# Moving the normalised tokens to the upper end of the SBUF partition, and the context, mixed and MLP features down beside the weight tiles

## The chip, the cores and the metric

The kernel runs on one core of a Trainium2 chip. The metric is the device time of one execution in microseconds (us). The kernel before took 2857.2 us (median of three runs, 2851.56 to 2862.92).

## The reference

One layer of a diffusion backbone over 512 latent tokens and 256 context tokens of width 2048, all in float32. Cut to what matters:

```python
sh1, sc1, g1, sh2, sc2, g2 = split(silu(c) @ w_ada + b_ada)           # modulation vectors
u_lat = rmsnorm(x) * (1 + sc1) + sh1                                  # 512 tokens ("normalised tokens")
u_ctx = rmsnorm(ctx) * (1 + csc1) + csh1                              # 256 tokens ("context")
p_lat, p_ctx = u_lat @ w_in, u_ctx @ w_in                             # 8192 columns
a_lat = hgrn2(p_lat[:, :5120], p_ctx[:, :5120])                       # 8 heads, both directions
y_lat = hyena(p_lat[:, 5120:])                                        # long convolution by transform matrices
x = x + g1 * (concat(a_lat, y_lat) @ w_out)                           # "mixed features"
u2 = rmsnorm(x) * (1 + sc2) + sh2
x = x + g2 * (square(relu(u2 @ w_mlp1)) @ w_mlp2)                     # hidden width 8192 ("MLP features")
out = rmsnorm(x)
```

## The kernel before, in words

TensorE works in three products per float32 product. `wsplit` (L198) and its like split each operand into a rounded part `hi` and the exact rest `lo`, and every product is hi·hi + hi·lo + lo·hi: `mm3` (L249 to L252), or the three lines L1022 to L1024 and L1102 to L1104. Each of these matmuls loads a stationary tile of 128 x 128 and streams a moving tile of 512 columns (256 for the context) past it; the accumulators are PSUM banks.

A weight tile `raw` (512 KB, 128 x 1024) is loaded by SyncE's queue, rounded by ScalarE (`whi`, L202) and split by VectorE (`wlo`, L149), three in flight at each step (`Stream`). The stages follow each other:

- head (to about 160 us): modulation of x, filter of the long convolution; the normalised tokens `uT0` to `uT15` are made, one tile of 4 KB per partition for each block of 128 features (hi 2 KB, lo 2 KB).
- Hyena (to about 540 us): projections of `uT`, transforms with the matrices `mat`, `mati`, `fsd`, `ff`.
- HGRN (to about 1228 us): for each head a query and a gate (`project`, of `uT` alone) and three projections of both `uT` and the context `uc` (`project2`, three `uT` matmuls and three `uc` matmuls in turn).
- output projection (to about 1406 us): weights stream as the moving side, the mixed features `mix0` to `mix15` are the stationary side; `OUT_PLAN` goes through mix8 to 15 (`Y_ROWS`) and mix0 to 7 (`A_ROWS`) in turn.
- MLP (to about 2836 us): eight rounds; in each, first `u2 @ w_mlp1` (L1080, stationary `whi`/`wlo`, moving `u2`), then `h @ w_mlp2` (L1102 to L1104, stationary `h`, moving `whi`/`wlo`), 384 matmuls each.

In `mm3(ps, wh, wl, xh, xl, ..)` the second argument of `pe.matmul` is the stationary side and the third the moving side. The profile's operand pairs don't tell the roles, which are taken from the code: in rows of L250 to L252 with `uT`, `u` or `uc`, that tile is moving; in rows of L1022 to L1024 and L1102 to L1104, `mix` and `h` are stationary; of `mat,pq` the moving one is `mat`; of `fsd,mat` and `ff,mat` the stationary one is `mat`.

SBUF is shared out by pools, which are stacked from the left (low addresses) or from the right (high addresses) of each partition. The pools of this change: A holds `uT`, later mix0 to 7, later `u2` (and for a while the odd filter groups' `ff`); YM holds `uc`, later mix8 to 15, later `h`; W holds `raw`, `whi`, `wlo`. M holds `mat`, Y `mati`, `ue`, `uo` and `pq`.

```python
    MP = pool("M", side=right)
    mat = MP.tile([P, 2, 4, 2, 256], F32R, name="mat")
    AP_ = pool("A")
    WP = pool("W")
    HP = pool("H", side=right)
```

Of the kernel before, what the change touches and what calls it, by code (L numbers as in the profile page):

```python
# [29 lines left out]
RAW, WB = 3, 3  # weight tiles in flight as loaded and as split  # L30
MISC_QUEUE = "scalar"
NPRE, PRE_CTX = 2, 0  # heads whose query and gate come first; the one after which the context is prepared
K_QUEUE = "sync"
P_QUEUE = "gpsimd"
FILTER_AT = {0: (0, 1, 2, 3)}  # channel groups of the filter after a step of the modulation
# how far instructions move up or down in the order of issue
# [5 lines left out]
SIDE = 114  # weight tiles over which the later modulation vectors are spread  # L42
# [25 lines left out]
def stream_order():  # L68
    """Weight tiles of [128, 1024] in the order of their use: (weight, first row, first column, k blocks)."""
    r = []  # L70

    def half_cols(c0):
        r.extend(("w_in", hf * W, c0, 8) for hf in range(2))

    def pairs(w, rows, c0):
        r.extend((w, r0, c0, 2) for r0 in rows)

    for g in range(4):
        for n in range(3 if g == 0 else 0, 6):
            half_cols((5 + n // 2) * W + (2 * g + n % 2) * P)  # L80
    for h in range(NPRE):
        for part in (0, 4):
            half_cols(part * W + h * P)
    for h in range(H):
        for part in (1, 2, 3) + ((0, 4) if h >= NPRE else ()):
            half_cols(part * W + h * P)
    for ng, rows in OUT_PLAN:
        pairs("w_out", rows, ng * 512)
    for c in range(8):
        for f in (2 * c, 2 * c + 1):  # L90
            pairs("w_mlp1", range(0, D, 256), f * 512)
        for rep in range(1 if c < 7 else 2):
            for ng in range(4):
                pairs("w_mlp2", range(c * W, (c + 1) * W, 256), ng * 512)
    return r


def arrange(a):
    """The inputs as the kernel loads them: weights in tiles, vectors as columns."""
    f = np.float32  # L100
    k = constants()
    ada = a["w_ada"][0].reshape(P, 16, 6, D)
    order = list(dict.fromkeys(stream_order()))
    tiles = np.empty((len(order), P, 1024), f)
    for t, (w, r0, c0, nk) in zip(tiles, order):
        n = 1024 // nk
        t.reshape(P, nk, n)[:] = a[w][0][r0:r0 + nk * P, c0:c0 + n].reshape(nk, P, n).transpose(1, 0, 2)
    first = np.concatenate([a["w_in"][0][:, 5 * W:5 * W + 256], a["w_in"][0][:, 6 * W:6 * W + P]], axis=1)
    rows = lambda v: v.reshape(-1, P).T
    pad = lambda v: np.concatenate([v, np.zeros((P - v.shape[0],) + v.shape[1:], f)])  # L110
    twice = lambda v, axis: np.concatenate([v, v], axis=axis)
    fvec = np.stack([a["flt_b1"][0], a["flt_b2"][0], a["flt_freq"][0]], axis=1)
    head = [a["c"][0].reshape(P, 16), a["c_ctx"].reshape(P, 16), twice(fvec, 0), k["k_negt"], pad(a["flt_w1"][0]),
            pad(twice(a["flt_w2"][0], 1))]
    cols = [rows(a["b_ada"][0]), rows(a["norm1_g"][0]), rows(a["norm2_g"][0]),
            rows(a["hgrn_norm_g"][0]), rows(a["hy_conv_b"][0]), rows(a["hgrn_lb_logits"]), rows(a["hy_conv_w"][0]),
            rows(a["hy_bias"][0])]
    d = {"x": a["x"][0], "ctx": a["ctx"][0], "b_ada": a["b_ada"], "final_norm_g": a["final_norm_g"][None],
         "ada1": ada[:, :, 0:2].reshape(P, 8, 2, 2, 8, 256).transpose(4, 1, 0, 2, 3, 5).reshape(8, 8, P, 1024),
         "ada2": ada[:, :, 2:6].reshape(P, 16, 16, 512).transpose(2, 1, 0, 3),  # L120
         "first": first.reshape(8, 2, P, 384).transpose(0, 2, 1, 3).reshape(8, P, 768),
         "tiles": tiles, "head": np.concatenate(head, axis=1),
         "columns": np.concatenate(cols, axis=1),
         "flt_w3": twice(a["flt_w3"][0].reshape(64, 2, 4, 256).transpose(0, 2, 1, 3).reshape(64, 2, 1024), 0),
         "k_zt": k["k_zt"], "k_delta": k["k_delta"], "k_mats": k["k_mats"], "k_tri": k["k_tri"]}
    return {n: np.ascontiguousarray(v) for n, v in d.items()}
# [16 lines left out]
def body(nc, tc, A, out, stack, dbg, stop):  # L143
# [4 lines left out]
    right = "right"  # L148
# [31 lines left out]
    grow = DR.tile([2, D], F32, name="grow")  # L180
# [7 lines left out]

    MP = pool("M", side=right)
    mat = MP.tile([P, 2, 4, 2, 256], F32R, name="mat")  # L190
    AP_ = pool("A")
# [6 lines left out]
    def wsplit(raw, n=1024):  # L198
        """f32r parts of the first n columns: the rounded value and the exact rest."""
# [6 lines left out]
    class Stream:  # L206
        """Weight tiles [128, k, n], loaded and split ahead of their use."""
# [25 lines left out]
    class Side:  # L233
        """Tasks spread evenly over a number of weight tiles."""
# [19 lines left out]
    def rsqrt_small(v, scale, pl, tag, add=EPS):  # L254
        """v <- (v * scale + add) ** -0.5 for a few columns: square root, reciprocal and one Newton step."""
# [11 lines left out]
    def make_u(u, xp, t, scale, bias):  # L267
        """u[:, 0], u[:, 1] <- f32r parts of xp * scale + bias."""
# [4 lines left out]
    # ---------------- conditioning vectors  # L273
# [20 lines left out]
    def load_wa(p):  # L294
        """Modulation columns of pair p as eight tiles of two k rows: shift and scale, 256 columns each."""
# [9 lines left out]
    def load_k(p):  # L305
        """Rows of the first three projected blocks for k blocks 2 p, 2 p + 1."""
        raw = wraw()
        kdma(raw[:, 0:768], A["first"][p])
        return raw

    # ---------------- x: token tiles, normalised
# [3 lines left out]
    # ---------------- implicit filter of the long convolution (some tiles borrow the space of later uT blocks)  # L315
# [12 lines left out]
    def load_mats(dst, i0, n):  # L328
        """Transform matrices i0, i0 + 1, .. as pairs of f32r parts."""
# [7 lines left out]
    # the second layer comes out on both halves of the partitions, for two concurrent products with half of the rows  # L337
# [27 lines left out]
    def forward(banks, q, ut):  # L365
        """Sum q (cosine even, odd; sine even, odd tokens) of a token-major tile: [128 m, (2, 256 ch)]."""
# [18 lines left out]
    def filter_taps(g):  # L385
        """Taps of 256 channels, forward and backward, by token parity; the squares' sums go to rnf."""
# [34 lines left out]
    def filter_spectrum(g):  # L421
        """Transform of the taps of channel group g: sums and differences of the two directions."""
# [34 lines left out]
    # ---------------- modulation of x, two k blocks at a time  # L457
# [6 lines left out]
    def mod_pair(p):  # L464
        """Shift and gain of x and of the context for k blocks 2 p, 2 p + 1: four rows of the vectors at a
        time, each on its own strip of the array's columns."""
# [19 lines left out]
    def project_k(p):  # L486
        """Adds k blocks 2 p, 2 p + 1 to the first three projected blocks."""
# [28 lines left out]
    # lower bound of the forget gates: softmax over two logits  # L516
# [21 lines left out]
    # ---------------- modulation vectors of later stages  # L538
    def gemv(col0, fin, row):
        """Tasks of 512 columns from col0; fin gets four feature columns [128, 4], or with row a row [1, 512]."""  # L540
# [27 lines left out]
    def mod_vec(name, six, norm=None):  # L568
        """Column block `six` of the modulation, [128, 16]; with norm: norm * (1 + value)."""
# [13 lines left out]
    def mod_row(r, six):  # L583
        """Column block `six` of the modulation as row r of grow."""
# [25 lines left out]
    # ---------------- Hyena: projections, long convolution  # L610
# [14 lines left out]
    def hy_evac(g, n, ps, cv, ueo):  # L625
        """Convolved block n (v, v, x1, x1, x0, x0) of channel group g; u = x1 * v goes token-major."""
# [90 lines left out]
    # ---------------- HGRN: both directions of a head at a time  # L717
    YM = pool("YM", side=right)  # context, later the mixed features of w_out, later the hidden features
# [22 lines left out]
    def view(ap, h):  # L741
        """Column-major order of the latent grid for the upper heads."""
# [20 lines left out]
    # queries and gates of the first heads run while the context is prepared  # L763
    for h in range(NPRE):
        mdma(qscr[h], query(h))
        mdma(gscr[h], gate(h))
        if h == PRE_CTX:
            # context: normalised and modulated, feature-major
# [24 lines left out]
    def project2(ps, pc):  # L793
        """Latent and context columns; the context follows two blocks behind."""
# [12 lines left out]
    def head(h):  # L807
        dirs = []
        for di, nm in enumerate("fb"):
# [10 lines left out]
            # cumulative log decay within chunks; for the context the sum over the tokens still to come  # L820
# [33 lines left out]
        # values  # L854
# [15 lines left out]
        # state that the context leaves  # L870
# [23 lines left out]
        # scores, transposed, two chunks at a time on the two halves of the array's columns; both directions  # L894
        # join block-diagonal matrices of two chunks
# [15 lines left out]
        for i in range(NCH):  # L911
            ns = i, NCH - 1 - i
            if i < NCH - 1:
                us = [0, 0]
                for di, n in enumerate(ns):
                    b_ = n % 2  # each half of the rows has its own bank
# [16 lines left out]
        # gate and readout  # L933
# [37 lines left out]
    # ---------------- output projection, residual, second norm; token-major  # L971
# [19 lines left out]
    def residual(pl, ps, i, ng, ssq):  # L991
        """x1 += row * ps for token tile i and column group ng; the squares' sum goes to ssq."""
# [8 lines left out]
    def rstd(pl, v, n, tag):  # L1001
        """[128, n, 4] sums of squares -> [128, n] reciprocal roots."""
# [48 lines left out]
    # ---------------- MLP  # L1051
# [8 lines left out]
    def final(i0):  # L1060
        """Output of token tiles i0, i0 + 1."""
# [62 lines left out]
```

## Time and profile before

| | |
|---|---|
| time, median of three runs | 2857.2 us (2851.56, 2857.20, 2862.92) |
| span of the profiled execution | 2851.5 us; the fastest of the three runs took 2851.56 us |
| TensorE matmul busy | 2794.1 us, 98% of the span, 13444 matmuls |
| TensorE weight load busy | 2219.4 us, 78% |
| VectorE, ScalarE busy | 1399.7 us (49%), 926.7 us (32%) |
| DMA | 369.07 MB, mean 129 GB/s |
| chain that ended last | 91% TensorE |

A matmul's row has a start and a duration; the duration (0.39 us at 512 columns) holds its way through the array and overlaps the next one's. What a matmul costs in a stream is therefore read from start to start.

### The profile page before, as it was taken

To read this page: it belongs to the slowest core of one execution; us is meant where nothing else is said; L and a number is where in the kernel's file an instruction comes from. 1 tells how busy PE (TensorE), PEld (TensorE's weight loads), DVE (VectorE), ACT (ScalarE), POOL (GpSimd) and SP (SyncE) were. 2 spreads that over 40 slices of the span, in tenths; PEclk is the share of its full clock that TensorE was granted. 3 is DMA by queue.
4 is the path that set the end of the run, shared out by engine and by line. 5 is a ranking of instruction groups with operands and counts; after the bars stand their busy time and mean duration, and the time that the engine had idled before them with its cause. 6 is when DMAs were issued, how large, how long until landed. Compare 5 with 4: busy or idle time off the path is not lost.

```text
span 2851.5 us, 33241 instructions
## 1 busy us (share of the span) xinstructions
PE 2794.1 (98%) x13444; PEld 2219.4 (78%) x13444; DVE 1399.7 (49%) x2021; ACT 926.7 (32%) x1269; POOL 11.5 (0%) x26
## 2 busy tenths in 40 slices
PE   7999999999999999999999999999999999999997
PEld 2468788787888877878788888888888888888886
DVE  4447777655564656533434344243442434424446
ACT  5432222554344423522332131222312222122233
POOL 0000000000000000100000000000000000000000
PEclk9999999999999999999999999999999999999999
DMA  7576555713443354333232222322222222233245
GB/s 303 214 263 198 163 181 162 252 49 111 137 129 105 111 156 136 116 139 113 96 104 96 96 96 89 104 94 95 93 96 97 95 97 96 96 96 96 96 132 178
DMA packets 122405, 369.07 MB, mean 129 GB/s; under 512 B 13595, under 2 KB 13979, under 8 KB 120332
## 3 DMA queue, kind: packets, MB, share of 16 engines
q1 hardware_dynamic: 112608, 339.00, 36.5%
q10 hardware_dynamic: 7724, 18.78, 1.8%
q0 software_dynamic: 1920, 9.18, 0.9%
q8 instruction: 105, 1.72, 0.3%
q14 instruction: 48, 0.39, 0.0%
HBM read 353.52 MB, written 13.39 MB: 129 GB/s over the span
## 4 chain that ended last, share of the span: by engine, by line
PE 91%; DMA 4%; DVE 3%; ACT 1%; issue 1%; SPq 0%; DVEq 0%; ACTq 0%
PE bank L250 17%; PE bank L251 17%; PE bank L252 17%; PE bank L1103 8%; PE bank L1102 8%; PE bank L1104 8%; DMA ga<-ada_dram 2%; PE bank L1022 2%; PE bank L1023 2%; PE bank L1024 2%; PE bank L471 2%; PE bank L921 1%; PE bank L923 1%; DVE gacc L554 1%; PE bank L865 0%
## 5 line engine op out<-in xcount | busy, mean ns | idle before, releaser
L149 DVE TENSOR_TENSOR wlo<-raw,whi 128x1024 fp32r<-128x1024 f32 (+1 forms) x434 | 529.1, 1219 | 974.0 <-ACT whi L202 957.3
L202 ACT CAST whi<-raw 128x1024 fp32r<-128x1024 f32 (+1 forms) x434 | 453.7, 1045 | 1374.2 <-PE bank L251 656.6
L251 PE MATMUL bank<-uT,whi 128*128 128x512 f32 x1024 | 408.4, 399 | 0.0
L252 PE MATMUL bank<-uT,wlo 128*128 128x512 f32 x1024 | 406.7, 398 | 0.0
L250 PE MATMUL bank<-uT,whi 128*128 128x512 f32 x1024 | 406.7, 397 | 0.0
L1102 PE MATMUL bank<-whi,h 128*128 128x512 f32 x1024 | 404.7, 395 | 0.0
L1103 PE MATMUL bank<-wlo,h 128*128 128x512 f32 x1024 | 404.7, 395 | 0.0
L1104 PE MATMUL bank<-whi,h 128*128 128x512 f32 x1024 | 404.6, 395 | 0.0
L252 PE MATMUL bank<-u,wlo 128*128 128x512 f32 x1024 | 399.3, 390 | 0.0
L250 PE MATMUL bank<-u,whi 128*128 128x512 f32 x1024 | 399.1, 390 | 0.0
L251 PE MATMUL bank<-u,whi 128*128 128x512 f32 x1024 | 398.9, 390 | 0.0
L252 PEld LDWEIGHTS bank<-uT,wlo 128*128 128x128 f32 x1024 | 193.0, 189 | 50.5 <-issue 12.5
L1103 PEld LDWEIGHTS bank<-wlo,h 128*128 128x128 f32 x1024 | 192.1, 188 | 46.9
L1104 PEld LDWEIGHTS bank<-whi,h 128*128 128x128 f32 x1024 | 192.1, 188 | 46.8
L1102 PEld LDWEIGHTS bank<-whi,h 128*128 128x128 f32 x1024 | 192.0, 188 | 46.9
L250 PEld LDWEIGHTS bank<-u,whi 128*128 128x128 f32 x1024 | 192.3, 188 | 39.9 <-ACT u L270 0.3
L251 PEld LDWEIGHTS bank<-u,whi 128*128 128x128 f32 x1024 | 192.3, 188 | 39.7
L252 PEld LDWEIGHTS bank<-u,wlo 128*128 128x128 f32 x1024 | 192.4, 188 | 39.6
L250 PEld LDWEIGHTS bank<-uT,whi 128*128 128x128 f32 x1024 | 193.0, 189 | 36.2 <-issue 9.2
L251 PEld LDWEIGHTS bank<-uT,whi 128*128 128x128 f32 x1024 | 193.5, 189 | 32.9 <-issue 6.6
L554 DVE SCALAR_TENSOR_TENSOR gacc<-ga,sil,gacc 128x512 f32<-128x512 f32 x240 | 179.5, 748 | 65.5 <-DMA ga<-ada_dram 62.5
L250 PE MATMUL bank<-uc,whi 128*128 128x256 f32 x384 | 108.8, 283 | 1.1 <-ACT sf L814 1.1
(395 smaller groups left out, 2931.9 us busy)
## 6 DMA issues: line engine op xcount, KB each, us to landing
raw<-tiles_dram SPq DMA_DIRECT2D x426, 512.0 KB, 3.5
ga<-ada_dram SPq DMA_DIRECT2D x256, 256.0 KB, 3.5
wa<-ada_dram SPq DMA_DIRECT2D x64, 512.0 KB, 6.3
x<-x_dram SPq DMA_DIRECT2D x4, 1024.0 KB
kscr<-kt ACTq DMA_DIRECT2D x8, 512.0 KB
K<-kscr ACTq DMA_DIRECT2D x4, 1024.0 KB, 6.6
x<-x_dram POOLq DMA_DIRECT2D x4, 1024.0 KB, 9.3
out_dram<-x SPq DMA_DIRECT2D x16, 256.0 KB, 2.3
```

Of the source, the lines that this page charges most:

```text
L149: tt = lambda o, x, y, op: vec.tensor_tensor(out=o, in0=x, in1=y, op=op)
L202: act.copy(hi[:, :n], raw[:, :n])
L250: pe.matmul(ps, wh, xh, start=start, stop=False, skip_group_check=True)
L251: pe.matmul(ps, wh, xl, start=False, stop=False, skip_group_check=True)
L252: pe.matmul(ps, wl, xh, start=False, stop=stop_, skip_group_check=True)
L471: pe.matmul(gm[32 * j:32 * j + 32, :], sil[:, kk], w_[kk // 2][:, kk % 2].rearrange("p a n -> p (a n)"), start=kk < 4, stop=kk >= 12, skip ...
L554: vec.scalar_tensor_tensor(out=acc, in0=g, scalar=s, in1=acc, op0=ALU.mult, op1=ALU.add)
L1022: pe.matmul(ps, m[:, 0, sl], hi[:, k], start=first, stop=False, skip_group_check=True)
L1023: pe.matmul(ps, m[:, 0, sl], lo[:, k], start=False, stop=False, skip_group_check=True)
L1102: pe.matmul(psb[i], t[:, 0, sl], hi[:, k], start=first, stop=False, skip_group_check=True)
L1103: pe.matmul(psb[i], t[:, 0, sl], lo[:, k], start=False, stop=False, skip_group_check=True)
L1104: pe.matmul(psb[i], t[:, 1, sl], hi[:, k], start=False, stop=last, skip_group_check=True)
```

## The change

Pool A is opened first of the pools on the right side, so that it takes the top of the partition, and everything else on that side (M, H, Y, Q, R, E, F) moves down under it. W moves down into the place of A. YM is opened on the left side, right above W. Nothing else is changed but comments.

```diff
@@ body
+    AP_ = pool("A", side=right)
     MP = pool("M", side=right)
     mat = MP.tile([P, 2, 4, 2, 256], F32R, name="mat")
-    AP_ = pool("A")
     WP = pool("W")
     HP = pool("H", side=right)
@@ after close("Y"), close("M")
-    YM = pool("YM", side=right)  # context, later the mixed features of w_out, later the hidden features
+    YM = pool("YM")
     QP = pool("Q", side=right)
```

On all five engines the two programs have the same instructions in the same order with the same waits, 19049 in each; only the names and the addresses of tiles differ. The addresses of the built programs, in bytes from the start of the partition, and the rest that the first byte of the pool's large tiles leaves when divided by 64:

```
pool  tiles                         before            rest   after             rest
W     raw, whi, wlo, ga              86784 .. 131840    0     21248 ..  66304    0
A     uT; mix0-7; u2; ff (odd g)     21248 ..  86784    0    163808 .. 229344   32
YM    uc; mix8-15; h                196576 .. 229344   32     66304 ..  99072    0
M     mat                           212960 .. 229344   32    147424 .. 163808   32
Y     mati, ue, uo, pq              133088 .. 212960   32     67552 .. 147424   32
H     fsd, ff (even g), wa          139776 .. 212960   32     74240 .. 147424   32
```

The tiles in W, A and YM are each a multiple of 512 bytes long and the slices that matmuls read start at multiples of 512 bytes in them, so the rest of the pool is the rest of each operand. Pools Q, E, F and R keep their rests.

## Rows read from the trace of the kernel before

**Rows 1.** The page, parts 1, 2 and 4: busy time by engine, the span in 40 slices (tenths busy, granted TensorE clock), and the chain that ended last.

```profile
span 2851.5 us, 33241 instructions
PE 2794.1 (98%) x13444; PEld 2219.4 (78%) x13444; DVE 1399.7 (49%) x2021; ACT 926.7 (32%) x1269; POOL 11.5 (0%) x26
PE   7999999999999999999999999999999999999997
PEclk9999999999999999999999999999999999999999
PE 91%; DMA 4%; DVE 3%; ACT 1%; issue 1%; SPq 0%; DVEq 0%; ACTq 0%
```

**Rows 2.** Busy time in the stretches head, Hyena, HGRN, output projection, normalisation, MLP, end: length of the stretch, busy us (and instructions) of PE, PEld, DVE, ACT, POOL, granted clock, DMA share, GB/s.

```profile
0.00:156.00 156.00, 134.51 (x641) 62.76 (x641) 74.09 (x162) 74.55 (x108) 0.69 (x6) 0.99 0.70 262
156.00:540.00 384.00, 373.52 (x1829) 298.16 (x1829) 270.21 (x406) 117.25 (x164) 0.00 (x0) 1.00 0.62 202
540.00:1228.00 688.00, 684.96 (x3996) 553.47 (x3995) 391.84 (x658) 296.44 (x459) 8.19 (x15) 1.00 0.38 118
1228.00:1406.00 178.00, 177.16 (x772) 144.24 (x771) 58.00 (x63) 47.71 (x65) 2.62 (x5) 1.00 0.36 123
1406.00:1421.00 15.00, 7.93 (x43) 6.39 (x42) 11.72 (x29) 10.59 (x20) 0.00 (x0) 0.77 0.32 116
1421.00:2836.00 1415.00, 1415.00 (x6168) 1153.90 (x6168) 584.43 (x687) 378.54 (x450) 0.00 (x0) 1.00 0.31 101
2836.00:2851.00 15.00, 0.98 (x5) 0.46 (x3) 9.46 (x21) 1.65 (x5) 0.00 (x0) 0.67 0.42 140
```

**Rows 3.** The timeline of PE at the borders of two MLP stages: start, duration, engine, line, operands. Between the first border and the second lie the 384 matmuls of one `h @ w_mlp2`, between the second and the third the 384 of the next `u2 @ w_mlp1`.

```profile
1510.52 0.40 PE L252 MATMUL bank<-u,wlo 128*128 128x512 f32 x1
1510.75 0.39 PE L1102 MATMUL bank<-whi,h 128*128 128x512 f32 x1
...
1600.12 0.39 PE L1104 MATMUL bank<-whi,h 128*128 128x512 f32 x1
1600.34 0.39 PE L250 MATMUL bank<-u,whi 128*128 128x512 f32 x1
...
1687.16 0.40 PE L252 MATMUL bank<-u,wlo 128*128 128x512 f32 x1
1687.39 0.39 PE L1102 MATMUL bank<-whi,h 128*128 128x512 f32 x1
```

**Rows 4.** The timeline of PE in the output projection, first at matmuls whose stationary side is of mix8 to 15 (YM), then of mix0 to 7 (A), as `OUT_PLAN` orders them; ten matmuls from the first row of each pair to its second.

```profile
1237.89 0.39 PE L1024 MATMUL bank<-whi,mix 128*128 128x512 f32 x1
...
1240.22 0.40 PE L1022 MATMUL bank<-whi,mix 128*128 128x512 f32 x1
...
1289.88 0.39 PE L1023 MATMUL bank<-wlo,mix 128*128 128x512 f32 x1
...
1292.14 0.39 PE L1024 MATMUL bank<-whi,mix 128*128 128x512 f32 x1
```

**Rows 5.** The timeline of PE at matmuls of 256 columns that all stand on tiles of rest 32 on the stationary side: eleven with `ff` of filter group 3 (A) moving past `mat`, then twelve with `mat` moving past `pq`. The last row of each pair is the start of the matmul behind them.

```profile
149.50 0.28 PE L251 MATMUL bank<-ff,mat 128*128 128x256 f32 x1
...
150.78 0.39 PE L250 MATMUL bank<-uT,whi 128*128 128x512 f32 x1
...
253.37 0.28 PE L250 MATMUL bank<-mat,pq 128*128 128x256 f32 x1
...
254.81 0.28 PE L252 MATMUL bank<-mati,pq 128*128 128x256 f32 x1
```

**Rows 6.** The timeline of PE in two heads' projections: from the first row to the second three `uT` matmuls that lie between `uc` matmuls; from the third to the fourth nine `uc` matmuls of 256 columns without a `uT` one between them.

```profile
578.72 0.39 PE L250 MATMUL bank<-uT,whi 128*128 128x512 f32 x1
...
579.41 0.28 PE L250 MATMUL bank<-uc,whi 128*128 128x256 f32 x1
...
724.21 0.28 PE L250 MATMUL bank<-uc,whi 128*128 128x256 f32 x1
...
725.27 0.39 PE L250 MATMUL bank<-uT,whi 128*128 128x512 f32 x1
```

**Rows 7.** The page, part 5, the groups of matmuls and of weight loads: line, engine, operation, operands, count, then busy us, mean ns of one, idle us before them. Each group is one of three lines with the same count.

```profile
L251 PE MATMUL bank<-uT,whi 128*128 128x512 f32 x1024 | 408.4, 399 | 0.0
L1102 PE MATMUL bank<-whi,h 128*128 128x512 f32 x1024 | 404.7, 395 | 0.0
L250 PE MATMUL bank<-u,whi 128*128 128x512 f32 x1024 | 399.1, 390 | 0.0
L1022 PE MATMUL bank<-whi,mix 128*128 128x512 f32 x256 | 100.4, 393 | 0.8 <-DVE m L952 0.8
L1104 PEld LDWEIGHTS bank<-whi,h 128*128 128x128 f32 x1024 | 192.1, 188 | 46.8
L252 PEld LDWEIGHTS bank<-u,wlo 128*128 128x128 f32 x1024 | 192.4, 188 | 39.6
L250 PE MATMUL bank<-uc,whi 128*128 128x256 f32 x384 | 108.8, 283 | 1.1 <-ACT sf L814 1.1
```

**Rows 8.** The matmuls that read `uT`, in Hyena and in HGRN, and then those that read `uc`, in HGRN: stretch, length, busy us (and count), granted clock, DMA share, GB/s.

```profile
156.00:540.00 384.00, 302.00 (x1277) 1.00 0.62 202
540.00:1228.00 688.00, 478.41 (x1730) 1.00 0.38 118
...
540.00:1228.00 688.00, 189.20 (x1152) 1.00 0.38 118
```

**Rows 9.** Who waited for whom in Hyena: engine, what, on what, then us in total, times, longest.

```profile
DVE gacc L554 <- DMA ga<-ada_dram: 42.1, 28, 3.0
ACT whi L202 <- DMA raw<-tiles_dram: 10.1, 3, 4.4
```

## The prediction

> **What bounds the kernel now.** I read the busy times and the slices first [rows 1]: TensorE is busy 98% of the span, its clock stands at the full level (2.4 GHz) in every slice, and 91% of the chain that ended last is TensorE's. The reader is to see that nothing but the number of matmuls and what one costs can move this time by much. The windows by stage [rows 2] say where that holds: in the MLP (1415 us) PE has no idle time, in HGRN (688 us) 3 us, in the output projection (178 us) 1 us, in Hyena 10.5 us, in the head 21.5 us.
>
> Then I read the price of a matmul, start to start, in each stage, because a busy PE does not say at what pace it goes. One `h @ w_mlp2` goes from 1510.75 to 1600.34, 89.59 us for 384 matmuls or 233.3 ns each; the `u2 @ w_mlp1` behind it goes from 1600.34 to 1687.39, 87.05 us for 384 or 226.7 ns each [rows 3]. Both have 512 columns, both read weight tiles as one side, neither waits. The output projection shows the same two prices with only one thing exchanged: with mix8 to 15 as the stationary side ten matmuls take 2.33 us (233 ns), with mix0 to 7 they take 2.26 us (226 ns) [rows 4]. The moving side is `whi` and `wlo` in both, the lines are the same three. What differs is the pool: YM against A. In YM tiles start 32 bytes past a multiple of 64, in A on a multiple of 64. I call a tile of rest 32 *shifted*. A shifted stationary tile costs 6.6 ns per matmul of 512 columns.
>
> The load of the stationary tile itself is not longer: 188 ns with `h`, 188 ns with the weights [rows 7]. The price shows only in the pace of the stream.
>
> For the moving side the trace has a pair at 256 columns, both with a shifted stationary tile: with `ff` of A (not shifted) moving, 11 matmuls take 1.28 us, 116.4 ns each; with `mat` (shifted) moving, 12 take 1.44 us, 120.0 ns each [rows 5]. A shifted moving tile costs 3.6 ns there; I take 3.3 ns, half of 6.6, since 116.7 is half of the 233.3 of a shifted stationary tile at 512 columns, and 120.0 is one such step above it. By columns that is 6.6 ns at 512.
>
> **What the change does.** It removes, adds and moves no instruction and no wait; every engine has the same rows in the same order. It exchanges the rests: A becomes shifted, YM stops being shifted, all others stay as they are. So the sum is over matmuls that read A or YM. Counts are from [rows 7, 8].
>
> 1. `h @ w_mlp2`, 3 x 1024 matmuls, stationary side no longer shifted: 3072 x 6.6 ns = 20.3 us less. PE has no idle time there, so it is all on the path. The price is the row's own.
> 2. `u2 @ w_mlp1`, 3 x 1024 matmuls, moving side now shifted: at 6.6 ns, 20.3 us more, all on the path. This pairing (stationary tile not shifted, moving tile shifted, 512 columns) has no row. Lower bound 0: the pair of [rows 5] was taken beside a shifted stationary tile and may not hold without one; a gain is left out, since no row shows a shifted tile at a quicker pace than an unshifted one. Upper bound 9.0 ns: `uc` is shifted, moves past unshifted weights, and nine of its matmuls take 1.06 us, 117.8 ns each [rows 6]; against the 113.3 that half of 226.7 would be, that is 4.5 ns at 256 columns. I take 6.6, the value of the pair in which only the moving tile differs.
> 3. The output projection: 384 matmuls get an unshifted stationary side, 384 a shifted one, each 6.6 ns. Sum 0.
> 4. `uT` in Hyena's stretch: 1277 matmuls x 6.6 ns = 8.4 us. Here PE waits 10.5 us of 384, and the waits behind it are transfers (VectorE waits 42.1 us for the modulation weights `ga`, and its splits of weight tiles queue behind that [rows 9]). A slower PE gives the transfers time, so a part is absorbed: I take three quarters, 6.3 us. Bounds: 0 (all 8.4 lie under the 10.5 us) and 8.4.
> 5. `uT` in HGRN: 1730 matmuls, of which the 24 projections with context (3 for each of 8 heads, 16 blocks of 3 matmuls each) have 1152 and queries and gates 578. The 578 alone: 3.8 us. The 1152: 7.6 us, less what `uc` gains by not being shifted, 1152 x 3.3 ns = 3.8 us, so 3.8 us more. That gain is less sure: beside `uc` the three `uT` take 0.69 us, 230 ns each instead of 226.7 [rows 6], so the turn from one kind to the other costs something too, and stays.
> 6. `uT` in the head: 3072 - 1277 - 1730 = 65 matmuls, 0.4 us, hidden: PE is idle 21.5 of 156 us there. Without that cover it would cost these 0.4 us. What VectorE and ScalarE read and write at shifted places is taken as 0 too: in the MLP they are busy 584 and 379 of 1415 us [rows 2], so that they could take twice as long under the cover of PE.
>
> Sum: -20.3 + 20.3 + 0 + 6.3 + 3.8 + 3.8 = +13.9 us. The profiled execution had a span of 2851.5, the fastest of the three runs; on it the forecast is 2865. The median of the runs is 5.7 us above, so on the median it is 2871.
>
> **A rule that speaks against it.** The Trainium skill ("TensorE: Matmul & The Clock Gate", Part 2, on loading the stationary operand) says that PE has two independent SBUF read ports and that loading the next tile's weights doesn't steal read bandwidth from the running matmul. "SBUF — State Buffer" (Specifications) gives lines of 16 bytes, of which 32 and 64 are both multiples. By these two no start in question should matter and the sum would be 0, 2857. The trace disagrees for the stationary side: 233 against 226 ns [rows 4]. It has no row for the third case in step 2.
>
> **Rivals.**
>
> *A shifted moving tile costs nothing past unshifted weights.* Then steps 2, 4 and 5 fall away, with `uc`'s gain, and only step 1 stays: -20.3, 2837 on the median; faster. For it: no row shows this pairing against its own unshifted counterpart. Against it: `mat` against `ff` [rows 5], and `uc` [rows 6], which with only its moving side shifted goes no quicker (117.8) than `ff` with only its stationary side shifted (116.4). The point from which it decides: per ns of moving price steps 2, 4 and 5 come to 3.07 + 0.96 + 0.58 + 1.15 = 5.8 us, step 1 gives 20.3 and `uc` 3.8, so the sum falls below 0 where the price is under 24.1 / 5.8 = 4.2 ns (3.5 if `uc` gains nothing).
>
> *The moving price is per matmul, not per column*: 3.3 ns at 512 columns too. Then -20.3 + 10.1 + 3.2 + 1.9 + 0 = -5, 2852; no change that can be told.
>
> *The moving price is what `uc` shows*, 9.0 ns: -20.3 + 27.6 + 8.6 + 5.2 + 10.4 - 3.8 = +28, 2885; slower.
>
> *The start of a tile is not the cause at all.* Something that goes with `h` and mix8 to 15 (what else is written into that pool, say) makes the 6.6 ns and stays: 0, 2857. Against it: the same line of the code writes mix0 to 6 and mix8 to 15, and `h` is written and read by others; the slow ones share only the pool. A variant: it is not the rest by 64 but the upper half of the partition (all shifted tiles above lie from 133088 up). Then A, which goes up, pays the same as in my sum, YM gains the same, and `mati`, `ue` and `uo` come down and gain under 1 us: the forecast stays.
>
> **How the numbers follow.** Chances: my sum 0.45, moving side free 0.17, per matmul 0.13, as `uc` shows 0.15, no effect 0.10. About 0.5%, 14.3 us, is what a measurement of this kernel can tell from no change, and my sum ends right at it, so its chance is divided between same and slower. Slower: 0.15 + 0.27 = 0.42. Faster: 0.17. Same: the rest, 0.41. The range goes from the free moving side to the `uc` case, each with some us for the runs' scatter: 2835 to 2888; the likeliest case alone, with step 4 at its bounds and `uc`'s gain between 0 and 4.5 ns, is 2863 to 2877.
>
> **What would show it.** In the timeline of the changed kernel: `h @ w_mlp2` in 87.05 us per 384 matmuls (step 1), `u2 @ w_mlp1` in 89.6 (step 2; 87.05 if the moving side is free, 90.5 if it is as `uc` shows), output projection with mix0 to 7 at 233 ns and mix8 to 15 at 226 (step 3), `ff` of filter group 3 past `mat` at 120.0 instead of 116.4. Hyena's stretch should grow by less than 8.4 us, with PE idle for less than 10.5 (step 4), HGRN's by 7.6 us (step 5). I am wrong if the two MLP stages don't change places, above all if `u2 @ w_mlp1` keeps its 87.05.

## The result: slower by 6 us, not by 14

The kernel after takes 2861.63 us (median of 20 runs, 2857.96 to 2871.61), the kernel before on the same chips 2855.45 us (20 runs, 2851.42 to 2863.04). The ratio is 1.0026, 95% interval 1.0017 to 1.0035: 5 to 10 us slower, 0.3%, less than the 0.5% that the prediction called noise. The forecast was +13.9 us.

### The profile after

The page of the kernel after, parts 1 and 5, against [rows 1, 7]:

```profile
span 2864.3 us, 33241 instructions
PE 2808.1 (98%) x13444; PEld 2223.4 (78%) x13444; DVE 1399.2 (49%) x2021; ACT 927.0 (32%) x1269; POOL 11.5 (0%) x26
...
L250 PE MATMUL bank<-u,whi 128*128 128x512 f32 x1024 | 405.6, 396 | 0.0
...
L1102 PE MATMUL bank<-whi,h 128*128 128x512 f32 x1024 | 398.4, 389 | 0.0
```

The same instructions, the same share of PE, and the means of `u` and `h` have changed places (390 to 396 and 395 to 389). The timeline of PE at three MLP borders, against [rows 3]; from the first row to the second lies one `h @ w_mlp2`, to the third the next `u2 @ w_mlp1`:

```profile
1525.91 0.40 PE L1102 MATMUL bank<-whi,h 128*128 128x512 f32 x1
...
1612.95 0.40 PE L250 MATMUL bank<-u,whi 128*128 128x512 f32 x1
...
1702.56 0.39 PE L1102 MATMUL bank<-whi,h 128*128 128x512 f32 x1
```

87.04 and 89.61 us: the two products have exchanged their prices. So have the halves of the output projection. Ten matmuls of mix8 to 15, then ten of mix0 to 7, against [rows 4]:

```profile
1251.83 0.39 PE L1022 MATMUL bank<-whi,mix 128*128 128x512 f32 x1
...
1254.10 0.39 PE L1023 MATMUL bank<-wlo,mix 128*128 128x512 f32 x1
...
1291.67 0.39 PE L1022 MATMUL bank<-whi,mix 128*128 128x512 f32 x1
...
1294.01 0.39 PE L1023 MATMUL bank<-wlo,mix 128*128 128x512 f32 x1
```

2.27 and 2.34 us, where it was 2.33 and 2.26. Three `uT` and three `uc` matmuls in turn, from the first row to the third, against [rows 6]:

```profile
719.00 0.40 PE L250 MATMUL bank<-uT,whi 128*128 128x512 f32 x1
...
719.70 0.28 PE L250 MATMUL bank<-uc,whi 128*128 128x256 f32 x1
...
720.05 0.40 PE L250 MATMUL bank<-uT,whi 128*128 128x512 f32 x1
```

1.05 us, as before (578.72 to 579.77 there, 0.69 of it for the `uT`). Here is the first sign of what was mis-sized.

The two spans shown, 2851.5 and 2864.3 us, lie 12.8 us apart, twice the 6 us of the runs. Windows of the head and of 30 us in HGRN (stretch, length, PE, PEld, DVE, ACT, POOL, granted clock, DMA share, GB/s), first of after, then of before:

```profile
0.00:156.00 156.00, 133.37 (x623) 62.08 (x623) 73.65 (x161) 74.01 (x107) 0.70 (x6) 0.96 0.68 253
770.00:800.00 30.00, 30.00 (x157) 22.18 (x156) 17.33 (x35) 9.67 (x17) 0.00 (x0) 0.89 0.42 137
```

```profile
770.00:800.00 30.00, 30.00 (x174) 24.26 (x175) 19.29 (x35) 11.35 (x20) 0.00 (x0) 1.00 0.52 161
```

In the 30 us the clock was granted at 0.89 in the mean in the one and 1.00 in the other (1.00 is 2.4 GHz, and 1.2 GHz counts as 0.50), with PE busy throughout in both. This comes and goes from execution to execution, with the kernel before too (below). In the head it was 0.96 against 0.99 [rows 2]. Of the other profiles of this document `after_late_side`, `after_unshifted` and `w_ladder32` show 0.96 there too, and all the rest 0.99; in the four with 0.96 Hyena's first transpose starts at 208.5 to 208.9 us, in the rest at 203.6 to 204.7. Three of the four are among the four profiles with A on the right side; whether the change makes this more frequent is open. I use a second pair of profiles, in which both stretches were granted the same clock, for the sum by stage.

### The profile page after: what moved, and what is told of

It reads as the page before. It is cut to its first block, busy times and chain, and to the rows that moved or that the text cites. A ratio compares the mean times of both kernels' runs of the same rounds, so it can differ in the third digit from the quotient of the medians.

```text
span 2864.3 us, 33241 instructions
## 1 busy us (share of the span) xinstructions
PE 2808.1 (98%) x13444; PEld 2223.4 (78%) x13444; DVE 1399.2 (49%) x2021; ACT 927.0 (32%) x1269; POOL 11.5 (0%) x26
## 4 chain that ended last, share of the span: by engine, by line
PE 93%; DMA 2%; DVE 2%; ACT 1%; issue 1%; SPq 0%; DVEq 0%; ACTq 0%
PE bank L250 18%; PE bank L252 18%; PE bank L251 18%; PE bank L1102 8%; PE bank L1104 8%; PE bank L1103 8%; PE bank L1022 2%; PE bank L1024 2%; PE bank L1023 2%; PE bank L471 2%; DMA ga<-ada_dram 1%; PE bank L921 1%; PE bank L923 1%; PE bank L865 1%; DVE gacc L554 0%
## 5 line engine op out<-in xcount | busy, mean ns | idle before, releaser
L250 PE MATMUL bank<-u,whi 128*128 128x512 f32 x1024 | 405.6, 396 | 0.0
L252 PE MATMUL bank<-u,wlo 128*128 128x512 f32 x1024 | 405.5, 396 | 0.0
L251 PE MATMUL bank<-u,whi 128*128 128x512 f32 x1024 | 405.2, 396 | 0.0
L1103 PE MATMUL bank<-wlo,h 128*128 128x512 f32 x1024 | 398.4, 389 | 0.0
L1102 PE MATMUL bank<-whi,h 128*128 128x512 f32 x1024 | 398.4, 389 | 0.0
L1104 PE MATMUL bank<-whi,h 128*128 128x512 f32 x1024 | 398.3, 389 | 0.0
```

The lines of the kernel that those rows point to most:

```text
L250: pe.matmul(ps, wh, xh, start=start, stop=False, skip_group_check=True)
L251: pe.matmul(ps, wh, xl, start=False, stop=False, skip_group_check=True)
L252: pe.matmul(ps, wl, xh, start=False, stop=stop_, skip_group_check=True)
L1102: pe.matmul(psb[i], t[:, 0, sl], hi[:, k], start=first, stop=False, skip_group_check=True)
L1103: pe.matmul(psb[i], t[:, 0, sl], lo[:, k], start=False, stop=False, skip_group_check=True)
L1104: pe.matmul(psb[i], t[:, 1, sl], hi[:, k], start=False, stop=last, skip_group_check=True)
```

## The experiments

None of these kernels changes what is computed. They change addresses of tiles, with a small memset for each pad, or when a transfer is issued; code lines stand up to seven further down in them. The stretch between MLP borders, 384 matmuls, is the measure: 87.05 us is the quick pace (226.7 ns), 89.6 the slow one (233.3 ns). The address of a tile is given modulo 256 from here on; W is at 0 unless said otherwise, in both kernels. Before, A (`uT`, `u2`) is at 0 and YM (`uc`, `h`) at 224; after, A is at 224 and YM at 0.

### Is it the rest by 64?

`all_unshifted` and `after_unshifted`: 32 bytes at the top of the right side, in the kernel before and in the kernel after, so that all of that side comes down to 192.

```diff
     state = pool("state")
...
+    XP = pool("X", side=right)
+    vec.memset(XP.tile([P, 8], F32, name="xpad"), 0.0)
```

> The kernel before with 32 bytes left free at the top of the partition, so that every pool on the right side starts 32 bytes lower: YM, M, Y and H get rest 0, A and W keep rest 0. Theory (the rest by 64 sets the price, on either side): h @ w_mlp2 in 87.05 us per 384 matmuls instead of 89.59 (-20.3 us), mix8 to 15 at 227 ns (-2.5), the 384 Hyena transform matmuls at 113.3 ns instead of 120 (-2.6), uc at 113 to 117 ns instead of 118 (-1 to -4): about 2827 us. Rival (something else about pool YM, or the upper half of the partition): all of these stay, 2855 us.

> The changed kernel with the same 32 bytes free at the top: A stays in the upper half but gets rest 0, as do M, Y and H; W and YM keep rest 0. Rest theory: u2 @ w_mlp1 and h @ w_mlp2 both in 87.05 us per 384, all of uT in HGRN at 227 ns where nothing is mixed in, the same time as the kernel before with all pools at rest 0, about 2827 us. Rival (the upper half of the partition is the slow one): u2 @ w_mlp1 stays at 89.6 us, uT at 233 ns, about 2859 us.

`a_shifted_low`: the kernel before, with 32 bytes opened below A and 32 below W, so that A is at 32 in the lower half, W at 64, YM still at 224.

> The kernel before with 32 free bytes ahead of pool A and 32 behind it: A stays in the lower half but gets rest 32, W and all else keep their rests (YM stays at 32). Rest theory: u2 @ w_mlp1 in 89.6 us per 384 (+20.3), all of the output projection at 233 ns (+2.5), uT dearer in HGRN by 6 to 11 us and in Hyena by 0 to 8 us: 2884 to 2897 us. Rival (upper half): no change, 2855 us.

`u2_ladder`: the kernel before with the `u2` tile of block kb starting 4·kb bytes late. The tiles are made 64 bytes longer for it, so the places of the sixteen themselves move as well: they lie at sixteen different addresses, one of them 0.

```diff
-        u = AP_.tile([P, 2, 512], F32R, tag=f"A{kb}", name=f"u2_{kb}")
+        u = AP_.tile([P, 1040], F32R, tag=f"A{kb}", name=f"u2_{kb}")[:, kb:kb + 1024].rearrange("p (a n) -> p a n", a=2)
```

> The kernel before with the tile of u2 for feature block kb starting 4 * kb bytes into its place, so that the sixteen moving tiles of u2 @ w_mlp1 have the rests 0, 4, 8, .. 60. If a moving tile pays for every line of 64 bytes that its reads straddle: rest 0 at 226.7 ns, all fifteen others dearer by about 6.6 ns, so 384 matmuls take 87.05 + 384 * 15/16 * 6.6 ns = 89.4 us. If the grain is 32 bytes: rests below 32 dearer too but rest 32 not, which the changed kernel has shown not to hold. If only the distance counts in steps of 16 bytes: rests 1 to 15 past a multiple of 16 dearer, the others by the two known prices.

Measured. The kernel before took 2854.82 us beside these. `all_unshifted` 2838.64 (ratio 0.9945, 0.9931 to 0.996); `after_unshifted` 2864.88 (1.0031, 1.0017 to 1.0045); `a_shifted_low` 2885.98 (1.0105, 1.009 to 1.0121); `u2_ladder` one run of 2885.99. The timelines of PE at three MLP borders (first `h @ w_mlp2`, then `u2 @ w_mlp1`), of `all_unshifted`:

```profile
1506.42 0.39 PE L1104 MATMUL bank<-whi,h 128*128 128x512 f32 x1
...
1594.31 0.39 PE L252 MATMUL bank<-u,whi 128*128 128x512 f32 x1
...
1681.35 0.39 PE L1104 MATMUL bank<-whi,h 128*128 128x512 f32 x1
```

of `after_unshifted`:

```profile
1526.40 0.39 PE L1104 MATMUL bank<-whi,h 128*128 128x512 f32 x1
...
1613.46 0.39 PE L252 MATMUL bank<-u,whi 128*128 128x512 f32 x1
...
1703.06 0.39 PE L1104 MATMUL bank<-whi,h 128*128 128x512 f32 x1
```

and of `a_shifted_low`:

```profile
1528.24 0.39 PE L1106 MATMUL bank<-whi,h 128*128 128x512 f32 x1
...
1617.83 0.39 PE L254 MATMUL bank<-u,whi 128*128 128x512 f32 x1
...
1707.42 0.39 PE L1106 MATMUL bank<-whi,h 128*128 128x512 f32 x1
```

`after_unshifted` decides: its `u2` is on a multiple of 64, and `u2 @ w_mlp1` still takes 89.60 us. My name for the cause, the rest by 64, falls. `a_shifted_low` decides on the variant: with A low in the partition `u2 @ w_mlp1` takes 89.59, so the upper half is not the cause either. And `all_unshifted` has a third pace, 87.89 us for `h` at 192. In `u2_ladder` the longer tiles also put `uT` at 0, 64, 128, 192 in turn, all on multiples of 64, and in Hyena they went at 232.5 ns in the mean. `u2 @ w_mlp1` took 89.38 us there. A price for straddled lines of 64 bytes had forecast 89.4, but any rule by which only the tile at 0 is quick gives nearly that, and the other three kernels speak against lines of 64.

What fits all four, and both kernels, is the distance of the two tiles of a matmul to each other (moving less stationary for `u2`, stationary less moving for `h`): where it is 0 modulo 256 the pace is always 226.7 ns.

### Is it the distance between the two sides?

`w_ladder32`: YM put at 0, and the split weight tiles of MLP round c start 32·c bytes late, so that one execution passes through all eight distances, on either side (`o` is the start in elements; one tile of Hyena has a buffer fewer, for the space).

```diff
-        hi = WP.tile([P, 1024], F32R, tag="whi", bufs=WB, name="whi")
-        lo = WP.tile([P, 1024], F32R, tag="wlo", bufs=WB, name="wlo")
+        hi = WP.tile([P, 1088], F32R, tag="whi", bufs=WB, name="whi")[:, o:o + 1024]
+        lo = WP.tile([P, 1088], F32R, tag="wlo", bufs=WB, name="wlo")[:, o:o + 1024]
```

> The kernel before with h and mix8 to 15 moved so that they lie a multiple of 256 bytes from the places of the weight tiles, as u2 does, and with the split weight tiles of MLP round c starting 32 * c bytes late. So in round c the stationary side lies 32 * c bytes above the moving side (modulo 256) in u2 @ w_mlp1, and as much below it in h @ w_mlp2; the eight rounds give sixteen prices. Theory now (the distance between the two sides, modulo 256, sets the price, not either start): round 0 at 87.05 us per 384 matmuls in both products; 89.6 at 32 and 224 in at least the two cases seen; 87.9 in h @ w_mlp2 with the stationary side 192 above. If the modulus is 128, round 4 is at 87.05 again; if 64, rounds 2, 4 and 6 too, which the last runs speak against. Old theory (rest by 64): even rounds 87.05, odd rounds 89.6 in both products.

`ym_on_w`: the kernel before, only with YM moved down by 224 bytes, to 0; the pools opened behind it move by 256, which changes no address modulo 256.

```diff
+    Z1 = pool("Z1", side=right)
+    vec.memset(Z1.tile([P, 56], F32, name="z1pad"), 0.0)
     YM = pool("YM", side=right)
+    Z2 = pool("Z2", side=right)
+    vec.memset(Z2.tile([P, 8], F32, name="z2pad"), 0.0)
```

> The kernel before with 224 bytes left free above pool YM and 32 below it, so that YM alone moves and lies a multiple of 256 bytes from the weight tiles, as A does. Distance theory: h @ w_mlp2 in 87.05 us (-20.3), mix8 to 15 at 227 ns (-2.5), the stretch with uc somewhere between the 1047 ns per six matmuls of before and the 1034 seen at a distance of 192 (0 to -4): 2855 - 23 to - 27, about 2830 us, quicker than with all pools at rest 0 (2839), where h @ w_mlp2 took 87.9. Old theory (rest by 64): -22 too, but then all pools at rest 0 should have been quicker than this one, not slower.

Measured. `ym_on_w` 2833.75 us against 2855.94 (0.993, 0.9917 to 0.9943); `w_ladder32` one run of 2869.66. The timeline of PE in `ym_on_w` at three MLP borders:

```profile
1506.99 0.39 PE L1106 MATMUL bank<-whi,h 128*128 128x512 f32 x1
...
1594.03 0.39 PE L250 MATMUL bank<-u,whi 128*128 128x512 f32 x1
...
1681.07 0.39 PE L1106 MATMUL bank<-whi,h 128*128 128x512 f32 x1
```

Both products are quick, 87.04 us, for the first time: eight times 2.55 us are 20.4 of the 22 us gained. In `w_ladder32` one `h @ w_mlp2` of round 0 (distance 0), and the borders of round 4 (distance 128):

```profile
1511.03 0.39 PE L1109 MATMUL bank<-whi,h 128*128 128x512 f32 x1
...
1598.08 0.39 PE L253 MATMUL bank<-u,whi 128*128 128x512 f32 x1
...
2136.02 0.39 PE L253 MATMUL bank<-u,whi 128*128 128x512 f32 x1
...
2225.26 0.40 PE L1109 MATMUL bank<-whi,h 128*128 128x512 f32 x1
...
2314.86 0.39 PE L253 MATMUL bank<-u,whi 128*128 128x512 f32 x1
```

In round 4 89.24 and 89.60 us, though all tiles start on multiples of 64. Round 0 takes 87.05 for `h @ w_mlp2`, rounds 1 to 7 89.2 to 90.0 us for either product. So of the steps of 32 only 0 is quick.

All this would also come out if each tile had to start on a multiple of 256 by itself: no run puts both tiles of a 512-column matmul at one address other than 0. A finer reading speaks for the distance. In the traces' times to the nanosecond, `u2 @ w_mlp1` at 224 and 0 (`after`), 32 and 64 (`a_shifted_low`) and 0 and 32 (round 1 of `w_ladder32`), all at distance 224, goes in one and the same alternation of steps, 235 ns and 231 or 232; at 192 and 0 (`after_unshifted`) and 0 and 64 (round 2), both at distance 192, it goes in another, 233, 233, 234. So the distance is seen in how the slow streams go, with `h` at 192 as the one exception (last section); that distance 0 is quick at any address is likely and not shown.

`w_ladder4`: the same with 4·c bytes.

> As the ladder in steps of 32 bytes, with steps of 4: in MLP round c the split weight tiles start 4 * c bytes late, all else lies a multiple of 256 bytes from their places. Which distances under 32 bytes cost something? If only whole steps of 32 bytes count, all sixteen stages take 87.05 us per 384 matmuls. If any distance that is not a multiple of 256 costs, all but round 0 are dearer, by about 2.5 us. If the grain is 16 bytes, rounds 1 to 3 stay near 87.05 or lie between, and rounds 4 to 7 are at 89.6.

Measured: one run of 2861.52 us. The borders of round 1 (4 bytes; first `u2 @ w_mlp1`, then `h @ w_mlp2`) and of the last `h @ w_mlp2` (28 bytes, to the start of its last matmul, 383 steps):

```profile
1596.39 0.40 PE L253 MATMUL bank<-u,whi 128*128 128x512 f32 x1
...
1685.62 0.40 PE L1109 MATMUL bank<-whi,h 128*128 128x512 f32 x1
...
1776.50 0.40 PE L253 MATMUL bank<-u,whi 128*128 128x512 f32 x1
...
2757.55 0.40 PE L1109 MATMUL bank<-whi,h 128*128 128x512 f32 x1
...
2844.59 0.39 PE L1111 MATMUL bank<-whi,h 128*128 128x512 f32 x1
```

Four bytes already cost: 89.23 and 90.88 us. But the price doesn't grow evenly: by 4, 8, .. 28 bytes `u2 @ w_mlp1` took 89.23, 88.58, 88.32, 89.59, 89.60, 88.75, 89.60, and `h @ w_mlp2` 90.87, 89.49, 87.89, 88.96, 90.67, 89.59 for 384 steps and, at 28, 87.04 for 383, 227.3 ns each and nearly as quick as at 0 (226.7). I have no explanation for the last.

### Where did the expected cost in Hyena and HGRN go?

`before_late_side` and `after_late_side`: in either kernel the transfers of `ga` are issued from HGRN on and no longer in Hyena, which takes away one wait under which a slower PE can hide.

```diff
-    S.side = Side(gem_lat, SIDE)
...
     QP = pool("Q", side=right)
+    S.side = Side(gem_lat, 72)
```

> The kernel before with the transfers and sums of the later modulation vectors (ga) taken out of Hyena and spread over HGRN. Read is the stretch from the first transpose of Hyena to the first of the context, 335.3 us before. It should lose most of the 10.8 us that TensorE waits there in gaps over 0.6 us: about 326 us. HGRN may get longer; the whole time is not what is compared.

> The changed kernel with the same transfers taken out of Hyena. If the waits for these transfers absorbed most of the dearer uT matmuls (1145 of them in a row of their kind, 5.9 ns each, 6.7 us), then without them Hyena's stretch is 5.5 to 6.7 us longer than in the kernel before with the same edit; if the waits had nothing to do with it, the difference is the 2.7 us seen between the two profiles (335.3 and 338.0), or less.

Measured: one run each, 2850.76 and 2865.88 us. Hyena from its first transpose (L639) to the first transpose of the context (L788), timeline of PE, before_late_side, then after_late_side (in brackets the idle time ahead, and on what):

```profile
204.28 0.27 PE L639 MATMUL bank<-ident,vc 128*128 128x128 f32 x1
...
528.94 0.45 PE L788 MATMUL bank<-ident,t1f 128*128 128x128 f32 x1 [4.72 <-DMA ga<-b_ada_dram]
```

```profile
208.86 0.27 PE L639 MATMUL bank<-ident,vc 128*128 128x128 f32 x1
...
538.37 0.45 PE L788 MATMUL bank<-ident,t1f 128*128 128x128 f32 x1 [3.74 <-DMA ga<-b_ada_dram]
```

324.66 against 329.51 us: 4.85 us come through without those transfers, less than the 5.5 to 6.7 expected if the waits absorbed most, and more than the 2.4 with the transfers (next). Each is one profile, and the same stretch took 335.32 us in the first profile of the kernel before, 2.5 us more than in its second, so these two numbers alone decide nothing. Without the wait ahead of L788, in brackets, the stretches are 319.94 and 325.77 us, a difference of 5.83, where with the transfers it is 0.39 (331.84 and 332.23, next) or 2.21 (in the first pair of profiles). So it is likely that the waits on `ga` absorb a large part; single profiles do not show it beyond their scatter. The 15 us between the two runs hold more than Hyena: 4.6 of the head, with its clock at 0.99 and 0.96, and 4.9 of HGRN, which has these transfers now (690.24 to 695.17).

`before_again` and `after_again`: the two kernels unchanged, profiled once more on one chip.

> The kernel before, unchanged, for a second profile: how much of the differences between the stages of the two profiles is scatter. MLP stages 87.05 and 89.59 us and the six uT and uc matmuls at 1047 ns again, to a tenth; HGRN 682.9 us plus half of what time its clock stands at half speed; Hyena 329 to 335 us.

> The changed kernel, unchanged, for a second profile. MLP stages 89.6 and 87.06 us and the six matmuls at 1047 ns again; HGRN some 2 to 3 us over the kernel before once the time at half clock is taken out; Hyena 3 to 6 us over it.

Measured: 2854.5 and 2861.11 us, spans 2852.5 and 2858.9. In this pair the clock shows 0.89 at 770 to 800 us in both. The timeline of PE where stages begin (Hyena, first transpose of the context, first projection with context, output projection, normalisation), of `before_again` and of `after_again`:

```profile
203.58 0.27 PE L639 MATMUL bank<-ident,vc 128*128 128x128 f32 x1
...
536.43 0.30 PE L788 MATMUL bank<-ident,t1f 128*128 128x128 f32 x1 [1.01 <-issue]
...
540.79 0.28 PE L250 MATMUL bank<-uc,whi 128*128 128x256 f32 x1
...
1228.53 0.39 PE L1022 MATMUL bank<-whi,mix 128*128 128x512 f32 x1
...
1413.99 0.48 PE L1040 MATMUL bank<-ident,xn 128*128 128x128 f32 x1 [7.07 <-DVE xn L1035]
```

```profile
203.76 0.27 PE L639 MATMUL bank<-ident,vc 128*128 128x128 f32 x1
...
538.99 0.45 PE L788 MATMUL bank<-ident,t1f 128*128 128x128 f32 x1 [3.00 <-issue]
...
544.74 0.28 PE L250 MATMUL bank<-uc,whi 128*128 128x256 f32 x1
...
1234.66 0.39 PE L1022 MATMUL bank<-whi,mix 128*128 128x512 f32 x1
...
1420.33 0.47 PE L1040 MATMUL bank<-ident,xn 128*128 128x128 f32 x1 [7.07 <-DVE xn L1035]
```

The 6.4 us of the spans are: head 0.2, Hyena 2.4 (332.85 to 335.23), the context's preparation on the turn to HGRN 1.4 (4.36 to 5.75), HGRN 2.2 (687.74 to 689.92), output projection 0.2, all behind it 0.1. Of Hyena's 2.4 us 2.0 are a longer wait ahead of L788, 3.00 us instead of 1.01.

### A version quicker than both

`uc_192`: `ym_on_w`, and the context's tiles 192 bytes late, since in `all_unshifted`, with `uc` there, three `uT` and three `uc` matmuls in turn took 1034 ns, against 1047 in both kernels and 1050 in `ym_on_w`.

```diff
-    ucp = [YM.tile([P, 2, 2, LC], F32R, tag=f"ym{8 + j}", name="uc") for j in range(KB // 2)]
+    ucp = [YM.tile([P, 1088], F32R, tag=f"ym{8 + j}", name="uc")[:, 48:1072].rearrange("p (k a n) -> p k a n", k=2, a=2)
+           for j in range(KB // 2)]
```

> The kernel in which YM lies on the places of the weight tiles, with the context tiles alone starting 192 bytes late in it: u2, h, mix and uT at distance 0 from the weight tiles, uc at 192, where three uT and three uc matmuls in turn took 1034 ns instead of 1050 at distance 0 and 1047 at 224. If distances set this price too, HGRN loses 288 groups of six * 16 ns = 4.6 us on the kernel with YM on W: 2833.8 - 4.6 = about 2829 us, the quickest so far. If the 1034 came of something else in that kernel, 2834.

Measured: 2825.38 us against 2854.19 (0.99, 0.9883 to 0.9916), the quickest of all. One such turn in its timeline of PE, 1.03 us:

```profile
716.38 0.39 PE L250 MATMUL bank<-uT,whi 128*128 128x512 f32 x1
...
717.41 0.39 PE L250 MATMUL bank<-uT,whi 128*128 128x512 f32 x1
```

HGRN took 681.7 us in its profile and 687.7 in that of `ym_on_w`; the clock was granted at 1.00 at 770 to 800 us in the first and 0.89 in the second, which is 30 x 0.11 = 3.3 of the 6 us, so some 2.7 us are the tiles', where 4.6 had been expected. Against the kernel before, the two are 28.8 and 22.2 us quicker, but they were timed on different chips: how much of the 6.6 us between them comes from the place of `uc` is not settled.

## Why the prediction was too high, step by step

The forecast was +13.9 us; the runs gave +6.2, the pair of profiles +6.4. Step 5 has 5.4 us of what is missing and step 4 2.5.

- **Steps 1 and 2** (-20.3 and +20.3): right to the tenth. 89.59 to 87.04 us and 87.05 to 89.61 us in each round, and the whole MLP within 0.1 us. The moving side costs what the stationary side does. The rivals that priced it at 0, at 3.3 ns and at 9.0 ns all fall by the 89.61.
- **Step 3** (0): right, +0.2 us, the halves exchanged.
- **Step 4** (+6.3, bounds 0 to 8.4): 2.4 us, and 1.4 more where the context is prepared, which I had not named. The price was there: `uT` matmuls that follow one another in Hyena went from 227.3 to 233.2 ns from start to start in the mean, 7.5 us for 1277. Two thirds of it was absorbed, where I had let a quarter be; without the `ga` transfers 4.85 us come through. How much of it the waits on `ga` take, and why the turn to HGRN grew, are open.
- **Step 5** (+7.6) is the term that was most mis-sized: 2.2 us. The 3.8 us for the 578 matmuls of queries and gates came to 2.5 (228.3 to 232.7 ns). The 3.8 us net for the 1152 beside `uc` did not come: I charged +6.6 for each `uT` and -3.3 for each `uc`, +9.9 ns for three and three, and such a turn takes 1047 ns before and after. 720 of the 1152 stand in turns like this. The other 432 stand in rows of nine and did get dearer, from 228.6 to 232.8 ns, some 1.8 us; with the 2.5 that is more than the 2.2 measured, and what took up the rest is open. The 0.69 us that I noted for three `uT` beside `uc` [rows 6] was the sign: those `uT` went at the slow pace already, with an address at which they are quick among themselves. I called that the cost of the turn and added the price on top, instead of reading that in these turns there was none left to pay.
- **Step 6** (0): right, 0.2 us in the head.
- **The pair of [rows 5]** gave no price. The forecast read 116.4 ns for `ff` past `mat` from eleven matmuls. Nine more of filter group 3, 2 us ahead of them in the same trace, took 1.07 us or 118.9 ns, and the same nine took 1.07 us in the kernel after (first pair of rows before, second after):

```profile
147.38 0.28 PE L250 MATMUL bank<-ff,mat 128*128 128x256 f32 x1
...
148.45 0.39 PE L252 MATMUL bank<-uT,wlo 128*128 128x512 f32 x1
...
151.56 0.28 PE L250 MATMUL bank<-ff,mat 128*128 128x256 f32 x1
...
152.63 0.40 PE L252 MATMUL bank<-uT,wlo 128*128 128x512 f32 x1
```

The eleven went from 116.4 to 119.1 ns; but in `ym_on_w`, where both tiles lie as in the kernel before, the eleven took 118.2 and the nine 116.7. So these short rows vary by some 2 ns with nothing moved, more than half of the 3.6 ns that I read from one of them. And `mat` past `pq`, both at 224 and so at distance 0, takes 120.0 [rows 5]: the rule from 512 columns does not hold at 256. That the pair gave the right 6.6 ns in step 2 was luck.
- **The cause** was named wrongly. In the two kernels A, YM and W lie so that rest 32 by 64 and distance 224 modulo 256 are the same thing, and a trace of one kernel could not tell them apart. Steps 1 to 3 survived because the change exchanges both at once. The rival "the start of a tile is not the cause" falls by `ym_on_w`, which moves nothing but starts, and its variant by `a_shifted_low`.

The rule that spoke against the change is that PE has two independent SBUF read ports and that loading weights takes no read bandwidth from the running matmul (the Trainium skill, "TensorE: Matmul & The Clock Gate", Part 2). What I took from it, that no start matters, does not hold here: 224 bytes of one pool alone take `h @ w_mlp2` from 89.59 to 87.04 us. Whether it is the two reads that meet, no run shows.

## What to carry to other kernels

Where a matmul stream bounds the kernel, compare its start-to-start pace among stages of the same shape: 3% between them can be a matter of where tiles start, and a pad of 224 bytes was worth 22 us of 2856 here. Put tiles that meet in 512-column float32r matmuls at the same address modulo 256, best both on a multiple of 256, the only such place tried here. A price read in uniform streams is not to be added up for streams in which operands of different pools take turns: read the mixed stream itself.

## What the runs showed of the hardware that was not expected

- A float32r matmul stream of 512 columns with a weight load for each goes at 226.7 ns where the stationary and the moving tile both start on a multiple of 256 bytes, and at about 233 ns where one of them starts 32, 64, .. 224 bytes later (`w_ladder32`); 4 bytes are enough for 89.2 to 90.9 us per 384 (`w_ladder4`).
- The distance alone doesn't fix the other paces: `h` at 192 with W at 0 takes 87.89 us (`all_unshifted`), `h` at 0 with W at 64, the same distance, 89.60 (round 2 of `w_ladder32`). What the two reads meet at inside the chip stays open.
- Three `uT` (512 columns) and three `uc` (256) in turn, by their distances from W: (0, 224) 1047 ns, (224, 0) 1047, (0, 0) 1050, (192, 0) 1053, (0, 192) 1034. The prices of the uniform streams don't give these: `uT` at 224 instead of 0 costs some 6 ns each among themselves, and three of them nothing here.
